# Feed-forward products by Winograd's scheme: where the sums of blocks are formed, and how the residual is added

## The chip, the core and the metric

The kernel runs on one core of a Trainium2 chip. A core has a matrix engine (TensorE, in the profile PE, with its weight loads as PEld), three elementwise engines (VectorE or DVE, ScalarE or ACT, GpSimd or POOL) and a queue engine that issues transfers (SyncE or SP). Each engine works off its own list of instructions in order and waits on semaphores for the others. The metric is device microseconds (us) for one execution.

## The reference

One step of a hybrid encoder layer over 512 prompt tokens and 8 x 16 sample tokens (640 columns in the kernel), width 2048, with token mixers, an output projection and then a convolutional gated feed-forward network. The change is in the last part:

```python
D_FF = (D_MODEL * 11 // 4) // 128 * 128        # 5632
def conv_ffn(h, conv_past, w_up, conv_w, w_down):
    gp, val = jnp.split(h @ w_up, 2, axis=-1)
    gc, conv_new = causal_conv(gp, conv_past, conv_w)       # width 3
    return (jax.nn.silu(gc) * val) @ w_down, conv_new
...
    x = x + jnp.concatenate([o_gdn, o_fox, o_lru], axis=-1) @ p['w_out'][l]
    f_out, ffn_conv_new = conv_ffn(rmsnorm(x, p['norm_ffn_g'][l]), ffn_conv, p['ffn_w_up'][l],
                                   p['ffn_conv_w'][l], p['ffn_w_down'][l])
    x = x + f_out
...
    return rmsnorm(x, p['final_norm_g']), [jnp.stack(lst) for lst in outs]
```

## The kernel before

The feature axis lies on the 128 partitions and the tokens on the free axis, in two halves of 320 columns (HALF). A float32 product is made of three float32r products: each operand is split into a rounded part (hi, "wh" for weights) and the rest (lo, "wl"), and hi*hi, hi*lo and lo*hi are added in PSUM. The mixers and the output projection (about the first 1,240 us of the trace) are untouched apart from the DMA scratch size.

The feed-forward products go by Winograd's form of Strassen's scheme with seven block products P1 to P7 instead of eight. One step of `wino`, a "pair", takes a 4-block weight A11, A12, A21, A22 of 128x128 each and a 4-block operand B11, B12, B21, B22 of 128x320 each; it needs the weight sums S1 to S4 and the operand sums T1 to T4, and issues 21 matmuls of 320 columns (7 products x 3 parts), in the order of `SEQP`. There are 520 pairs:

- `up(f)`, 44 times with 8 pairs each: gate and value of one feature tile. When the seven sums stand in PSUM they are combined into C11 to C22 (tile x for the gate, v for the value); the gate goes through the normalisation's correction `corr`, the convolution (`conv`, line 257) and silu, is multiplied with the value, and the result goes to the DRAM tensor hT by a DMA from GpSimd.
- `down(i, end)`, 32 "visits" with 168 pairs in all: the 8 output feature pairs are visited in turn in four rounds, each time with the pairs that have come since (list `ends`): 2, 3, 3, 4, 5, 6, 7, 8 pairs in the first round (38), 51 and 47 in the next two, and 7, 6, 5, 4, 4, 3, 2, 1 (32) in the last. Each visit adds its result to the residual, which is loaded from and stored to the DRAM tensor x2 by SyncE.
- `plain`, at the end: the last pair of k tiles without the scheme, the sums of squares, and `finish`, the final norm.

`wino_x` makes an operand's T's and splits all seven blocks into hi and lo ("x" tiles); `form0` calls it for the 8 operands of `up`, and `form` for the 21 operands ("hops") of `down`, one after the other between the pairs of the visits, since a visit of n pairs needs the first n hops. `wino_w` loads one pair's weights ("w", SyncE queue), makes the S's ("ws") and splits: `next_w` keeps three pairs ahead of the products, and `wh` and `wl` have three buffers each, so that the split for a pair waits until the matrix engine has done the pair three before it.

Before the change `wino_w` makes S1, S2 and S4 on GpSimd (lines 1047, 1049, 1052, one after the other, each needing the one before) and S3 on VectorE (1048); hi is made by ScalarE in two copies (1050, 1053) and lo by VectorE in two subtractions of 384 and 512 columns (1051, 1054). `wino_x` makes all T's on GpSimd (1013 to 1016). GpSimd also does the two multiplications by `corr` in `up` (1354, 1359) and three of the additions at the end of a visit of `down` (1415).

PSUM has eight banks for these products (`pf`); a group uses seven. The next group starts in the eighth and takes each of the others when its sum has been read, so it waits for VectorE's (and, for P1, ScalarE's) reads at the end of a group. Generators (`drive`) set which work is issued between which pairs, and a scheduler then sets the order of the instructions on each engine when the kernel is built.

## Time and profile before

| | |
|---|---|
| runs | 3004.94 us median of 3 (3001.29, 3005.12, 3004.94) |
| profiled execution | span 3000.6 us from the first to the last instruction; its whole time is not shown apart, and the fastest run lies 0.7 us above this span |
| mean granted TensorE clock | 0.983 |
| busy | PE 2888.2 us (96%), DVE 2315.5 (77%), ACT 1109.7 (37%), POOL 1631.7 (54%) |
| HBM | read 306.75 MB, written 59.39 MB, 122 GB/s over the span |

"Busy" is the union of an engine's instructions. A window's row gives the busy time of each engine within a stretch of the span, with the number of instructions in brackets (a few matmul records are missing), the granted clock and the share of the DMA engines. A row of a group gives how often an instruction occurred, its busy time, the mean nanoseconds of one, and the idle time of its engine just before it with the releaser. By the matmuls, `up` runs from about 1,240 to 2,330 us, `down` from there to about 2,940 us, `plain` and `finish` after it.

### The profile page before, as it was taken

To read this page: it belongs to the slowest core of one execution; us is meant where nothing else is said; L and a number is where in the kernel's file an instruction comes from. 1 tells how busy PE (TensorE), PEld (TensorE's weight loads), DVE (VectorE), ACT (ScalarE), POOL (GpSimd) and SP (SyncE) were. 2 spreads that over 40 slices of the span, in tenths; PEclk is the share of its full clock that TensorE was granted. 3 is DMA by queue.
4 is the path that set the end of the run, shared out by engine and by line. 5 is a ranking of instruction groups with operands and counts; after the bars stand their busy time and mean duration, and the time that the engine had idled before them with its cause. 6 is when DMAs were issued, how large, how long until landed. Compare 5 with 4: busy or idle time off the path is not lost. (4 is left out here: it accounts for less than half of the span.)

```text
span 3000.6 us, 54322 instructions
## 1 busy us (share of the span) xinstructions
PE 2888.2 (96%) x19927; PEld 2804.4 (93%) x19927; DVE 2315.5 (77%) x3976; ACT 1109.7 (37%) x2023; POOL 1631.7 (54%) x2367
## 2 busy tenths in 40 slices
PE   8999999999999999999999999999999789999997
PEld 7999999999999999999999999999999789999996
DVE  8746545645634537899999999999999988999888
ACT  4333323323322313444444443444444334434433
POOL 3312200310300014677777777777777988888775
PEclk9999999999999999999999999999999899999998
DMA  5123143134134745433333333333333555555443
GB/s 207 56 93 109 59 143 121 59 123 143 58 109 150 264 130 179 130 105 98 98 99 101 98 98 103 99 101 98 98 98 98 171 160 156 164 163 173 155 138 119
DMA packets 175772, 369.68 MB, mean 123 GB/s; under 512 B 20137, under 2 KB 25145, under 8 KB 175505
## 3 DMA queue, kind: packets, MB, share of 16 engines
q1 hardware_dynamic: 169088, 340.28, 36.4%
q0 software_dynamic: 6416, 25.94, 2.4%
q8 instruction: 156, 2.56, 0.4%
q14 instruction: 112, 0.91, 0.1%
HBM read 306.75 MB, written 59.39 MB: 122 GB/s over the span
## 5 line engine op out<-in xcount | busy, mean ns | idle before, releaser
L1077 PE MATMUL p<-x,wh 128*128 128x320 f32 x7280 | 1625.0, 312 | 45.0 <-DVE t L1412 31.9
L1077 PEld LDWEIGHTS p<-x,wh 128*128 128x128 f32 x7280 | 1230.5, 190 | 56.4 <-DVE t L1412 36.2
L1077 PE MATMUL p<-x,wl 128*128 128x320 f32 x3640 | 1138.9, 313 | 8.9 <-DVE wl L1054 5.2
L1077 PEld LDWEIGHTS p<-x,wl 128*128 128x128 f32 x3640 | 691.5, 190 | 19.9 <-DVE wl L1054 15.1
L1054 DVE TENSOR_TENSOR wl<-ws,wh 128x512 fp32r<-128x512 f32 x520 | 527.4, 1014 | 25.3 <-ACT wh L1053 25.2
L1051 DVE TENSOR_TENSOR wl<-w,wh 128x384 fp32r<-128x384 f32 x520 | 449.6, 865 | 73.4 <-ACT wh L1050 67.7
L1053 ACT CAST wh<-ws 128x512 fp32r<-128x512 f32 x520 | 321.6, 619 | 389.4 <-POOL ws L1052 340.1
L146 PE MATMUL d<-xh,whi 128*128 128x320 f32 x1536 | 396.8, 327 | 0.0
L1050 ACT CAST wh<-w 128x384 fp32r<-128x384 f32 x520 | 264.8, 509 | 330.0 <-issue 169.8
L1052 POOL TENSOR_TENSOR ws<-w,ws 128x128 f32<-128x128 f32 x520 | 352.7, 678 | 40.4
L146 PE MATMUL d<-xl,whi 128*128 128x320 f32 x1536 | 370.8, 310 | 0.0
L146 PE MATMUL d<-xh,wlo 128*128 128x320 f32 x1536 | 370.5, 310 | 0.0
L1047 POOL TENSOR_TENSOR ws<-w 128x128 f32<-128x128 f32 x520 | 284.1, 546 | 150.3 <-DVE wl L1054 144.0
L1049 POOL TENSOR_TENSOR ws<-ws,w 128x128 f32<-128x128 f32 x520 | 344.0, 662 | 37.5
L135 DVE TENSOR_TENSOR wlo<-raw,whi 128x512 fp32r<-128x512 f32 x230 | 175.1, 761 | 212.5 <-ACT whi L134 204.8
L134 ACT CAST whi<-raw 128x512 fp32r<-128x512 f32 x230 | 142.4, 619 | 405.9 <-PE d L146 354.1
L146 PEld LDWEIGHTS d<-xh,whi 128*128 128x128 f32 x1536 | 256.9, 190 | 9.5 <-issue 5.5
L146 PEld LDWEIGHTS d<-xl,whi 128*128 128x128 f32 x1536 | 262.6, 189 | 0.2 <-issue 0.2
L146 PEld LDWEIGHTS d<-xh,wlo 128*128 128x128 f32 x1536 | 262.7, 189 | 0.0
L1048 DVE TENSOR_TENSOR ws<-w 128x128 f32<-128x128 f32 x520 | 218.3, 426 | 13.2 <-DMA w<-in_w_down 0.7
L868 POOL COPY q<-t 128x128 f32<-128x128 f32 x24 | 12.1, 523 | 261.2 <-DVE t L220 139.8
L257 DVE SCALAR_TENSOR_TENSOR t<-t,prm,t 128x656 f32<-128x656 f32 (+1 forms) x136 | 138.4, 1017 | 6.5 <-ACT t L253 3.5
(395 smaller groups left out, 3513.5 us busy)
## 6 DMA issues: line engine op xcount, KB each, us to landing
w<-in_w_up SPq DMA_DIRECT2D x352, 256.0 KB, 2.6
raw<-in_w_in SPq DMA_DIRECT2D x196, 256.0 KB, 2.8
w<-in_w_down SPq DMA_DIRECT2D x184, 256.0 KB, 2.7
t<-x SPq DMA_DIRECT2D x74, 320.0 KB, 3.6
kc<-in_ckT SPq DMA_DIRECT2D x32, 512.0 KB, 5.0
vc<-in_cv SPq DMA_DIRECT2D x32, 512.0 KB, 5.8
x<-t SPq DMA_DIRECT2D x48, 320.0 KB, 2.2
hT<-t POOLq DMA_DIRECT2D x44, 320.0 KB, 2.5
```

The costliest lines, as they stand in the source:

```text
L134: nc.scalar.copy(hi[:, :n], raw[:, :n])
L135: nc.vector.tensor_sub(lo[:, :n], raw[:, :n], hi[:, :n].bitcast(F32))
L146: self.nc.tensor.matmul(ps[h][:, :HALF], wt[:, w], x[:, h * HALF:(h + 1) * HALF], start=start and i == 0, stop=stop and i == 2)
L1047: nc.gpsimd.tensor_add(s[:, 0], w[:, 0], w[:, 3])
L1048: nc.vector.tensor_sub(s[:, 2], w[:, 1], w[:, 0])
L1049: nc.gpsimd.tensor_sub(s[:, 1], s[:, 0], w[:, 1])
L1050: nc.scalar.copy(hi[:, 0:3], w[:, 1:4])
L1051: nc.vector.tensor_sub(lo[:, 0:3], w[:, 1:4], hi[:, 0:3].bitcast(F32))
L1052: nc.gpsimd.tensor_sub(s[:, 3], w[:, 2], s[:, 1])
L1053: nc.scalar.copy(hi[:, 3:7], s)
L1054: nc.vector.tensor_sub(lo[:, 3:7], s, hi[:, 3:7].bitcast(F32))
L1077: nc.tensor.matmul(ps[p], l[:, wi], r[:, xi], start=i == 0 and j == 0, stop=i == n - 1 and j == 2)
```

## The change

- The S's are made by VectorE alone, in place behind the loaded blocks of a wider w tile, in three instructions: two S's at once (128x256, one operand repeated), then two of 128x128 that each need the one before. The first row of blocks has the other sign (this shows in `combine` as subtractions), and the DRAM layout of the weights has another order of blocks. hi and lo are made of all seven blocks at once (one ScalarE copy and one VectorE subtraction of 128x896, where there were two of each). The S's and hi of the next pair are issued before lo of this one; raw weights are loaded further ahead (w has 5 buffers).
- The T's are made by VectorE, in three instructions, in a 7-block f tile (2 buffers, where there were 3 of 4 blocks); the split is in two pieces instead of three.
- `combine` is used by `up` and `down`. The two multiplications by corr move from GpSimd to VectorE.
- `down` no longer loads the residual. It combines into y and adds by an accumulating DMA from GpSimd: y onto x2 in DRAM, or in the last round x2 onto y in SBUF. Three GpSimd additions, one VectorE addition, 64 loads and 48 stores of SyncE per kernel go; 64 DMAs of GpSimd come.
- The DMA scratch of the GpSimd queue is 4096 instead of the default, and the load of the old convolution state fc0 is cut into four.

The order of the products, and the f tile:

```diff
-    SEQP = ((1, 0, 0), (6, 4, 5), (7, 5, 6), (5, 3, 4), (2, 1, 2), (4, 2, 1), (3, 6, 3))
+    SEQP = ((1, 2, 2), (6, 5, 6), (7, 4, 4), (5, 3, 5), (2, 0, 0), (4, 1, 3), (3, 6, 1))
...
-        return self.ffn.tile([P, 4, HALF], F32, tag="f", bufs=3, name=self.name("f"))
+        return self.ffn.tile([P, 7, HALF], F32, tag="f", bufs=2, name=self.name("f"))
```

`wino_x`:

```diff
-        nc.gpsimd.tensor_sub(t[:, 0], f[:, 1], f[:, 0])
-        nc.gpsimd.tensor_sub(t[:, 1], f[:, 3], t[:, 0])
-        nc.gpsimd.tensor_sub(t[:, 2], f[:, 3], f[:, 1])
-        nc.gpsimd.tensor_sub(f[:, 1], f[:, 2], t[:, 1])
+        nc.vector.tensor_tensor(f[:, 4:6], f[:, 3:4].to_broadcast([P, 2, HALF]), f[:, 1:3], op=OP.subtract)
+        nc.vector.tensor_sub(f[:, 6], f[:, 1], f[:, 5])
+        nc.vector.tensor_sub(f[:, 3], f[:, 0], f[:, 6])
...
+        for a, b in ((0, 3), (3, 7)):
+            nc.scalar.copy(h3[:, a:b], f[:, a:b])
+            yield
+            nc.vector.tensor_sub(l3[:, a:b], f[:, a:b], h3[:, a:b].bitcast(F32))
+            yield
```

The weights (`wino_raw` loads, `wino_w` sums and makes hi, `wino_lo` makes lo):

```diff
+    def wino_w(self, w, plain):
...
+        part = w[:, 0:4] if plain else w[:, 1:8]
+        if not plain:
+            nc.vector.tensor_tensor(w[:, 4:6], w[:, 0:1].to_broadcast([P, 2, P]), w[:, 2:4], op=OP.add)
+            nc.vector.tensor_add(w[:, 6], w[:, 4], w[:, 3])
+            nc.vector.tensor_add(w[:, 7], w[:, 1], w[:, 6])
...
+        nc.scalar.copy(hi[:, 0:n], part)
+        return part, hi, lo
...
+            now, raw = self.wn, self.next_raw()
+            self.wn = raw and self.wino_w(*raw)
+            self.wq.append(self.wino_lo(*now))
```

`combine`, for `up` and `down`:

```diff
+        nc.scalar.copy(u1, ps[1])
+        nc.vector.tensor_sub(u2, ps[6], u1)
+        nc.vector.tensor_add(c21, u2, ps[7])
+        nc.vector.tensor_add(u2, u2, ps[5])
+        nc.vector.tensor_add(c22, c21, ps[5])
+        c11(u1, ps[2])
+        nc.vector.tensor_add(c21, c21, ps[4])
+        c12(ps[3], u2)
```

`up`, then `down`:

```diff
-            nc.gpsimd.tensor_mul(x[:, 2:], x[:, 2:], corr[:, 2:])
+            nc.vector.tensor_mul(x[:, 2:], x[:, 2:], corr[:, 2:])
...
-            nc.gpsimd.tensor_mul(y[:, :656], y[:, :656], corr[:, 2:])
+            nc.vector.tensor_mul(y[:, :656], y[:, :656], corr[:, 2:])
...
-                nc.sync.dma_start(xs[e], x2[2 * i + e])
...
-            gadd(1, 1, u3)
-            gadd(1, 0, u3)
-            gadd(0, 1, u2)
-            if not last:
-                for e in range(2):
-                    nc.sync.dma_start(x2[2 * i + e], xs[e])
+                if last:
+                    nc.gpsimd.dma_start(y[e], x2[2 * i + e], accum_op=OP.add)
+                else:
+                    nc.gpsimd.dma_start(x2[2 * i + e], y[e], accum_op=OP.add)
```

GpSimd within one feature tile of `up`, before (t are the x, y and v tiles of `up`; ws the S's; the groups of three for the other pairs follow alike):

```order
L1354 TENSOR_TENSOR t_13241<-t_13241,corr 128x656 [waits DVE_49]
L1355 COPY ns_fc<-t_13241 128x2 [waits Pool_49]
L1356 COPY ns_fc<-t_13241 128x16
L1047 TENSOR_TENSOR ws_13345<-w_13344 128x128 [waits DMAHW1_49,DVE_49]
L1049 TENSOR_TENSOR ws_13345<-ws_13345,w_13344 128x128 [waits Pool_49]
L1052 TENSOR_TENSOR ws_13345<-w_13344,ws_13345 128x128 [waits Pool_49]
L1047 TENSOR_TENSOR ws_13379<-w_13378 128x128 [waits DMAHW2_49,DVE_49]
L1359 TENSOR_TENSOR t_13242<-t_13242,corr 128x656 [waits Activation_49]
```

and after, a whole feature tile:

```order
L1367 MEMSET t_18933 128x2 [waits DMASW4_49,Activation_49]
L1368 COPY t_18933<-ns_fc 128x8x2
L1380 COPY ns_fc<-t_18658 128x2 [waits DVE_49]
L1381 COPY ns_fc<-t_18658 128x16 [waits Pool_49]
L1392 DMA hT<-t_18660 128x640 [waits DVE_49]
```

All arithmetic has left the list; a memset, small copies and the DMA are what stays.

VectorE at the end of a feature tile of `up`, before (p are the PSUM sums, lines 1343 to 1352 the combining):

```order
L1048 TENSOR_TENSOR ws_21259<-w_21258 128x128 [waits DMAHW2_49,DVE_49]
L1051 TENSOR_TENSOR wl_21192<-w_21189,wh_21191 128x384 [waits PE_49,Activation_49]
L1054 TENSOR_TENSOR wl_21192<-ws_21190,wh_21191 128x512 [waits Activation_49]
L1347 TENSOR_TENSOR t_21224<-t_21224,p_20945 128x320 [waits PE_49,Activation_49]
L1048 TENSOR_TENSOR ws_21293<-w_21292 128x128 [waits DMAHW3_49,DVE_49]
L1348 TENSOR_TENSOR t_21225<-t_21224,p_20946 128x320 [waits DVE_49,PE_49]
L1343 TENSOR_TENSOR t_21223<-t_21224,p_20948 128x256 [waits DMASW6_49,PE_49]
L1349 TENSOR_TENSOR t_21224<-t_21224,p_20947 128x320 [waits DVE_49]
```

and after (lines 1106 to 1111 and 1374, 1375):

```order
L1047 TENSOR_TENSOR w_15573<-w_15573 128x256 [waits DMAHW4_49]
L1048 TENSOR_TENSOR w_15573<-w_15573 128x128 [waits DVE_49]
L1049 TENSOR_TENSOR w_15573<-w_15573 128x128 [waits DVE_49]
L1058 TENSOR_TENSOR wl_15579<-w_15483,wh_15578 128x896 [waits PE_49,Activation_49]
L1106 TENSOR_TENSOR t_15634<-p_15387,t_15634 128x320 [waits PE_49,Activation_49]
L1374 TENSOR_TENSOR t_15633<-t_15634,p_15390 128x256 [waits DMASW0_49,PE_49]
L1107 TENSOR_TENSOR t_15635<-t_15634,p_15388 128x320 [waits DVE_49]
L1375 TENSOR_TENSOR t_15633<-t_15634,p_15390 128x4x16
L1108 TENSOR_TENSOR t_15634<-t_15634,p_15389 128x320 [waits DVE_49]
L1109 TENSOR_TENSOR t_15635<-t_15635,p_15389 128x320
```

Three weight sums stand ahead of each lo, the later two directly behind what they need, as in 301 of 1,040 cases over the kernel; the combining is one block as before.

VectorE at the end of the first visit of `down`, before (t is the residual, u the sum of products):

```order
L1412 TENSOR_TENSOR t_26188<-t_26188,p_26192 128x320 [waits Activation_49]
L1418 TENSOR_TENSOR u_26283<-u_26283,p_26193 128x320
L1412 TENSOR_TENSOR t_26189<-t_26189,p_26195 128x320 [waits DMAHW7_49]
L1419 TENSOR_TENSOR u_26283<-u_26283,p_26194 128x320 [waits DVE_49]
L1412 TENSOR_TENSOR t_26188<-t_26188,p_26196 128x320
L1412 TENSOR_TENSOR t_26189<-t_26189,p_26197 128x320
```

and after, with the last of a hop's operand sums (f) ahead of it and weights for the next pairs behind it:

```order
L1022 TENSOR_TENSOR f_24828<-f_24828 128x320 [waits DVE_49]
L1106 TENSOR_TENSOR u_24836<-p_24756,u_24836 128x320 [waits PE_49,Activation_49]
L1047 TENSOR_TENSOR w_24690<-w_24690 128x256 [waits DMAHW1_49]
L1107 TENSOR_TENSOR t_24835<-u_24836,p_24757 128x320 [waits DMASW2_49,DVE_49,PE_49]
L1431 TENSOR_TENSOR t_24834<-u_24836,p_24759 128x320 [waits PE_49,Pool_49]
L1108 TENSOR_TENSOR u_24836<-u_24836,p_24758 128x320 [waits DVE_49]
L1109 TENSOR_TENSOR t_24835<-t_24835,p_24758 128x320
L1432 TENSOR_TENSOR t_24834<-p_24761,u_24836 128x320 [waits DVE_49,PE_49]
L1111 TENSOR_TENSOR t_24835<-t_24835,p_24760 128x320 [waits DVE_49]
L1048 TENSOR_TENSOR w_24690<-w_24690 128x128
L1058 TENSOR_TENSOR wl_24804<-w_24660,wh_24803 128x896
```

The wait for the residual's load (DMAHW) is gone; a wait for a GpSimd DMA that last read the y tile (DMASW) has come.

127 lines of the change are left out of this document (53 added, 74 removed).

## Prediction

> **What bounds the kernel now.** I read the page's busy rows first, then windows by stage, then the waits of the matrix engine, then the durations on VectorE.
>
> ```profile
> span 3000.6 us, 54322 instructions
> PE 2888.2 (96%) x19927; PEld 2804.4 (93%) x19927; DVE 2315.5 (77%) x3976; ACT 1109.7 (37%) x2023; POOL 1631.7 (54%) x2367
> DVE  8746545645634537899999999999999988999888
> POOL 3312200310300014677777777777777988888775
> PEclk9999999999999999999999999999999899999998
> ```
>
> The matrix engine is busy for 96%, and the change takes no matmul away. VectorE's 77% is a mean: from the 17th slice on, the feed-forward part, its digits are 8 and 9.
>
> ```profile
> core 0: us, PE busy (x) PEld busy (x) DVE busy (x) ACT busy (x) POOL busy (x), PEclk, DMA share, GB/s
> 1250.00:1300.00 50.00, 44.30 (x284) 42.55 (x284) 43.98 (x78) 21.91 (x38) 40.07 (x64) 0.97 0.30 88
> 1400.00:2200.00 800.00, 798.29 (x5398) 791.30 (x5397) 761.30 (x1252) 324.46 (x612) 616.68 (x998) 1.00 0.34 99
> 2320.00:2460.00 140.00, 112.78 (x658) 107.06 (x657) 129.08 (x189) 56.08 (x99) 126.42 (x156) 0.89 0.51 165
> 2460.00:2790.00 330.00, 309.99 (x2013) 304.00 (x2012) 296.12 (x445) 133.95 (x246) 280.41 (x380) 0.97 0.52 162
> 2790.00:2930.00 140.00, 140.00 (x957) 140.00 (x956) 118.75 (x210) 51.91 (x101) 102.25 (x162) 1.00 0.46 145
> ```
>
> In `up` (1400 to 2200) the matrix engine is full: 5398 recorded matmuls in 800 us, 0.148 us each, so a pair of 21 takes 3.11 us and a feature tile of 168 takes 24.9 us. That rate is the floor of every other stage. Against it 2320 to 2460 (the first round of `down`) lost 140 - 658 x 0.148 = 42.6 us, of which 27.2 are idle and the rest the clock of 0.89; 2460 to 2790 (second and third round) lost 330 - 2013 x 0.148 = 32.1; the start of `up` lost 50 - 284 x 0.148 = 8.0; the last round lost nothing. About 83 us can be had in all, 75 of them in `down`.
>
> ```profile
> engine line waited for: us in total, times, longest us
> PE p L1077 <- DVE t L1412: 31.9, 16, 3.5
> PE p L1077 <- ACT wh L1050: 5.1, 3, 2.3
> PE p L1077 <- DVE t L1347: 3.3, 1, 3.3
> PE p L1077 <- DVE wl L1051: 3.2, 4, 2.1
> ```
>
> These are the matrix engine's waits from 2320 to 2800. Most are for line 1412, VectorE's reading of a visit's sums out of PSUM, 16 times at about 2 us: VectorE, in order, comes to the end of a visit too late. GpSimd is in the same state there (126.42 of 140). So the question is whether VectorE with more work is done sooner.
>
> **VectorE's prices.** Seven rows with minimum, median and maximum of one line's instructions, and two groups of the window 1400 to 2200 with the mean behind the busy time:
>
> ```profile
> engine op xcount: duration ns min/median/max, first and last start us, forms
> L1054 DVE TENSOR_TENSOR wl<-ws,wh x520: 676/946/2114, 1227.0 to 2930.3; 128x512 fp32r<-128x512 f32 x174
> L1051 DVE TENSOR_TENSOR wl<-w,wh x520: 543/812/1760, 1226.5 to 2929.3; 128x384 fp32r<-128x384 f32 x174
> L1028 DVE TENSOR_TENSOR x<-f,x x29: 1145/1147/1408, 1156.3 to 2788.7; 128x960 fp32r<-128x960 f32 x29
> L1025 DVE TENSOR_TENSOR x<-f,x x29: 809/1080/1499, 1154.4 to 2786.3; 128x640 fp32r<-128x640 f32 x29
> L1412 DVE TENSOR_TENSOR t<-t,p x144: 472/475/482, 2363.6 to 2838.9; 128x320 f32<-128x320 f32 x144
> L1362 DVE TENSOR_TENSOR t<-t,t x88: 410/422/684, 1281.1 to 2368.5; 128x256 f32<-128x256 f32 x88
> L257 DVE SCALAR_TENSOR_TENSOR t<-t,prm,t x136: 895/982/1797, 58.1 to 2362.6; 128x656 f32<-128x656 f32 x88, 128x664 f32<-128x664 f32 x48
> L1343 DVE TENSOR_TENSOR t<-t,p 128x256 f32<-128x256 f32 x64 | 26.4, 412 | 0.0
> L1344 DVE TENSOR_TENSOR t<-t,p 128x64 f32<-128x64 f32 x64 | 13.6, 212 | 0.0
> ```
>
> Instructions that read two SBUF tiles spread widely (line 1054 from 676 to 2114 ns), those with an operand in PSUM not at all (line 1412 from 472 to 482). The timeline shows why:
>
> ```profile
> 1900.09 0.68 DVE L1054 TENSOR_TENSOR wl<-ws,wh 128x512 fp32r<-128x512 f32 x1
> 1900.80 0.29 DVE L1048 TENSOR_TENSOR ws<-w 128x128 f32<-128x128 f32 x1
> 1900.85 0.57 POOL L1047 TENSOR_TENSOR ws<-w 128x128 f32<-128x128 f32 x1 [1.38 <-DVE wl L1054]
> 1901.37 1.35 POOL L1359 TENSOR_TENSOR t<-t,corr 128x656 f32<-128x656 f32 x1
> 1901.39 1.74 DVE L1051 TENSOR_TENSOR wl<-w,wh 128x384 fp32r<-128x384 f32 x1 [0.30 <-ACT wh L1050]
> ```
>
> Line 1054 took 0.68 with GpSimd idle. Line 1051 began with GpSimd's 1.35 us multiplication and took 1.74, more than three times its 0.54 minimum: it waited the other out. With no arithmetic on GpSimd I take the minima: 128 columns 0.29, 256 columns 0.42, 640 columns 0.81, 960 columns 1.15. Between 512 (0.68) and 960 a column costs 1.05 ns, so 896 columns come to 1.08, 656 to 0.83, 320 from SBUF to 0.49, 1280 to 1.48. The upper bound is the medians under contention, which would add some 40%.
>
> The Trainium skill speaks against the change here: "Perfetto Trace Analysis", section Optimizing Scalar/DVE Operations, advises to move work from a saturated VectorE to ScalarE or even GpSimd. The same section warns that the two share a read port, so that this may not help, and "SBUF — State Buffer", section Who interferes with whom, says that an instruction with two SBUF inputs contends with a GpSimd instruction that reads SBUF. The trace agrees with the latter (0.68 against 1.74 in the rows above).
>
> A row's duration is also not what the queue pays:
>
> ```profile
> 2617.22 0.47 DVE L1412 TENSOR_TENSOR t<-t,p 128x320 f32<-128x320 f32 x1
> 2617.62 0.47 DVE L1418 TENSOR_TENSOR u<-u,p 128x320 f32<-128x320 f32 x1
> 1143.12 0.17 DVE L115 SCALAR_TENSOR_TENSOR s<-s,s 128x5 f32<-128x5 f32 x1
> 1143.32 0.17 DVE L117 SCALAR_TENSOR_TENSOR s<-s,s 128x5 f32<-128x5 f32 x1
> ```
>
> The second pair of sums starts 0.40 after the first: an independent instruction costs its duration less 0.07 or 0.08. Line 117, which needs what line 115 just wrote, starts 0.03 after its end. So a direct dependence costs 0.11 more; 301 of the 520 pairs' 1040 short sums stand so in the order, 0.06 us a pair.
>
> **The change, part by part.** *A pair's weights on VectorE:* 0.42 + 0.29 + 0.29 + 1.08 = 2.08, less 4 x 0.077, plus 0.06: 1.83 us. The three old lines in 2320 to 2790 took 1.03, 0.83 and 0.56 (groups of that window, next fence), 2.30 with the overlaps taken off. More work, less time, because the contention goes.
>
> ```profile
> L1054 DVE TENSOR_TENSOR wl<-ws,wh 128x512 fp32r<-128x512 f32 x127 | 131.0, 1032 | 18.5 <-ACT wh L1053 18.5
> L1051 DVE TENSOR_TENSOR wl<-w,wh 128x384 fp32r<-128x384 f32 x128 | 106.2, 829 | 17.8 <-ACT wh L1050 17.8
> L1048 DVE TENSOR_TENSOR ws<-w 128x128 f32<-128x128 f32 x127 | 68.6, 559 | 1.6
> ```
>
> *`up`.* A tile: 8 weights 16.6; combining 5 x 0.475 + 2 x 0.41 + 2 x 0.21 = 3.6; the two multiplications by corr 1.66; the convolution's two steps 1.8; the products with the gate 2 x 0.42 + 2 x 0.21 = 1.3. That is 25.0 in 49 instructions; less 49 x 0.077, plus 0.5 for dependences: 21.7 of 24.9 us, 87%, where the window shows 95% (761.30 of 800). `up` lost 1.7 us in 800 at 95%, so it stays bound by the matrix engine, gaining 1 to 2 us. Combining keeps its place and releases the banks within about 3 us as before.
>
> *`down`.* Combining is 7 x 0.40 = 2.8 us on VectorE (8 x 0.40 before). A hop costs 0.81 + 0.49 + 0.49 + 1.15 + 1.48 less 5 x 0.077, 4.0 us; before, its three subtractions alone were about 3.1. Second and third round: 98 pairs x 1.83 + 16 visits x 2.8 + 13 hops x 4.0 = 276 us against 98 x 3.11 = 305 for the matrix engine, 90%. By the old prices it was 98 x 2.30 + 16 x 3.2 + 13 x 3.1 = 317: VectorE was the bound, and stops being it. I leave 5 of the 32.1 us for visits with a hop of their own: plus 27. First round: 38 x 1.83 + 8 x 2.8 + 7 x 4.0 = 120 against 118; the short first visits are the worst, since the last feature tile's combining, a visit's combining and a hop (11 us of VectorE and more) fall on 6 us of matmuls. Following the order through the first five visits I find stalls of about 3, 2, 1, 1 and 1 us, and as much again for the slower clock behind them: 16 of the 42.6 stay, plus 26 or 27. For the clock, the Trainium skill ("TensorE: Matmul & The Clock Gate", part 1) has it halve only after an idle window of some 3.4 us; by that these short stalls would cost themselves alone, an estimate of 8 us better. The windows disagree: 0.97 from 2460 to 2790 with no listed stall above 3.5.
>
> *Start of `up`, 1140 to 1300.* Eight hops bring 8 x 1.6 = 13 us more onto VectorE, and the slowed subtractions get faster by about as much; 0, between -5 and +5. *ScalarE:* one copy of 896 columns instead of 509 + 619 ns, less in all; nothing, its cover is its 59% of idle time. *SyncE:* 112 transfers fewer and two reloads of a tile more, hidden behind three pairs of raw weights ahead (9 us).
>
> *Accumulating DMAs.* No row shows one. Nearest:
>
> ```profile
> hT<-t POOLq DMA_DIRECT2D x44, 320.0 KB, 2.5
> t<-x SPq DMA_DIRECT2D x74, 320.0 KB, 3.6
> ```
>
> A store takes 2.5 us to land, a load 3.6; bounds 2.5 and, read and write in turn twice over, 12. The y tile is written again two visits later, at least 15 us in the first round, so both ends cost nothing; a gain isn't in it either, as no VectorE row waited for the old loads. At the end the last tile lands 3 us of combining plus 3 to 12 after the last visit, and is read after 7 x 12 matmuls, 12.4 us: 0, at worst 4 lost. The smaller scratch and the cut load lie on GpSimd, which has 46% idle already: 0, at worst 3.
>
> *Sum:* 27 + 26.5 + 1.5 + 0 = 55 us. The profiled span 3000.6 becomes 2946; the runs' median 3004.94, 4.3 above that span (the fastest run 0.7), becomes 2950.
>
> **Rivals.** *VectorE becomes the bound of `up`* (slower). It decides at the overlap: 25.0 us in 49 instructions stay under 24.9 only while each starts at least a few ns before the last one's end. If waits made each cost +0.03 as behind line 115, a tile took 26.5: 44 x 1.6 = 70 us, and `down` would gain nothing: 3075. For it: nearly all new instructions carry a wait. Against it: line 1418 has waits too and overlaps.
>
> *The contention isn't what goes* (slower, same mechanism from another cause): at the old medians lo costs 0.95 + 0.81 and the sums 0.43 each, a pair 3.2 and a tile above 33 us; 44 x 8 = 350 more. That gives 3355. The 1.74 us row speaks against it. The advice of the Trainium skill's "Perfetto Trace Analysis" quoted above would come out here, were its warning not true.
>
> *`down` stays bound by VectorE.* If hops and combining still collide, only half of the 75 comes: 20 to 35 gained, about 2977. For it: the first round is 120 against 118, and GpSimd and VectorE together lost more there than sums of either explain.
>
> *Accumulations land late.* From 15 us on, the early visits wait; at 30 us visits 3 to 5 lose some 14 + 11 + 5, and 25 us of gain are left: 2980. Nothing in the rows above comes near.
>
> *All stalls go*, the start's too: 83 gained, 2922.
>
> **How the numbers follow.** Forecast (35 to 70 gained) 0.64; `down` half bound 0.14; all gone 0.10; `up` bound 0.05; contention stays 0.02; late accumulations 0.05. Two tenths of a per cent, 6 us, is about what a measurement of this kernel can tell. Faster holds the forecast, all gone, most of the half-bound and of the late case: 0.90; same 0.03; slower the two VectorE cases: 0.07. The range takes the forecast and half-bound cases and part of all gone: 2925 to 2985.
>
> **What would show it.** In the profile after: VectorE's lo of 896 columns near 1.08 us with a narrow spread, the 320-column PSUM rows still 0.475; VectorE near 87% in `up` with 0.148 us per matmul; the waits for a visit's reading of PSUM in `down` under 15 us instead of 32; matmuls of 2320 to 2460 up from 658 towards 850; the clock there back above 0.95; accumulating stores landing under 12 us. Wrong would make it: a lo above 1.3 us, VectorE above 97% in `up`, or waits for the GpSimd queue ahead of the combining.

## The result, and the profile after

The changed kernel takes 2919.55 us (median; 2916.72 to 2920.93), the kernel before 3005.03 on the same chip: a ratio of 0.9716, with a 95% interval of 0.9702 to 0.973. The forecast was 2950 with a range from 2925: the sign was right, but 85 us came where 55 were promised, and the measured time lies just under the range.

The page after, its busy rows and three of the slice rows:

```profile
span 2918.3 us, 51439 instructions
PE 2851.7 (98%) x19927; PEld 2781.9 (95%) x19927; DVE 2179.0 (75%) x4610; ACT 1057.5 (36%) x1474; POOL 411.3 (14%) x574
DVE  8746644635644445898888889988888999988877
POOL 4311310301310001010111101110101010000014
PEclk9999999999999999999999999999999999999998
```

GpSimd's digits of 7 and 8 have become 0 and 1, the clock row has lost all but its last 8, and VectorE is a little less busy although it took over most of GpSimd's sums. The windows that the prediction used, after:

```profile
core 0: us, PE busy (x) PEld busy (x) DVE busy (x) ACT busy (x) POOL busy (x), PEclk, DMA share, GB/s
1250.00:1300.00 50.00, 48.01 (x325) 47.15 (x324) 46.90 (x110) 22.09 (x26) 7.55 (x16) 1.00 0.37 111
1400.00:2200.00 800.00, 800.00 (x5457) 800.00 (x5456) 707.81 (x1593) 305.56 (x358) 84.21 (x162) 1.00 0.35 100
2320.00:2460.00 140.00, 136.01 (x906) 133.92 (x906) 137.53 (x286) 61.57 (x69) 16.50 (x20) 0.99 0.66 164
2460.00:2790.00 330.00, 327.62 (x2189) 320.75 (x2188) 284.79 (x593) 126.95 (x143) 29.73 (x34) 1.00 0.57 138
```

Look at the second row first. In 800 us of `up` there are now 5457 matmuls, 59 more than before, though PE's busy time was 798.29 then and is 800.00 now. So a matmul takes 0.1466 us (0.1467 as the mean over the 42 tiles below), a pair 3.08, a tile 24.64, and the 0.148 us that the prediction took for the floor contained lost time. PE's busy row hid it: a matmul is shown as 0.31 us long, with a modelled end, while the next one starts 0.147 us after it, so a start that comes 0.1 us late leaves no gap. The PEld row showed it: 791.30 of 800 before, 800.00 now. From 2320 to 2460 the window holds 906 matmuls instead of 658, at a clock of 0.99 instead of 0.89, and VectorE is still full there (137.53 of 140).

VectorE's prices (line, tiles, shape, count, then busy time and mean ns of one, then idle time before them):

```profile
L1058 DVE TENSOR_TENSOR wl<-w,wh 128x896 fp32r<-128x896 f32 x520 | 567.0, 1090 | 115.5 <-ACT wh L1053 74.0 <-PE p L1094 40.5
L1047 DVE TENSOR_TENSOR w<-w 128x256 f32<-128x256 f32 x520 | 218.8, 423 | 53.5 <-DMA w<-in_w_down 49.6 <-DMA w<-in_w_up 3.2
L1048 DVE TENSOR_TENSOR w<-w 128x128 f32<-128x128 f32 x520 | 149.6, 290 | 4.1
L1032 DVE TENSOR_TENSOR x<-f,x 128x1280 fp32r<-128x1280 f32 x29 | 43.3, 1492 | 0.0
L1379 DVE TENSOR_TENSOR t<-t,corr 128x656 f32<-128x656 f32 x44 | 37.1, 843 | 0.0
L1109 DVE TENSOR_TENSOR t<-t,p 128x320 f32<-128x320 f32 x68 | 32.9, 484 | 0.0
```

They are the forecast ones within 2%: 1.09 for 1.08 us (896 columns), 0.42, 0.29, 1.49 for 1.48, 0.84 for 0.83, and 0.484 for 0.475 with an operand in PSUM. The matrix engine's waits for VectorE and ScalarE in the scheme's products, from 2290 to 2900, longest groups:

```profile
PE p L1094 <- DVE u L1106: 2.9, 4, 0.9
...
PE p L1094 <- ACT wh L1053: 2.3, 1, 2.3
```

Before, VectorE's reading of PSUM alone was waited for 31.9 us in a shorter stretch. Where the gain came from is seen best by stages. The matmul records of both traces are complete for the scheme's products (10920 in each), so the start of each stage is the start of the matmul with that number; "limit" is the stage's number of matmuls at 0.1467 us.

| stage, us | limit | before | after | gain | forecast |
|---|---|---|---|---|---|
| up to the first tile of `up` | - | 1232.9 | 1228.7 | 4.2 | 0 |
| first tile of `up` | 24.6 | 34.7 | 29.6 | 5.1 | 0 |
| 42 tiles of `up` | 1034.9 | 1047.5 | 1035.1 | 12.4 | 1.5 |
| last tile of `up` and first round of `down` | 141.6 | 189.2 | 149.0 | 40.2 | 26.5 |
| second and third round | 301.9 | 333.1 | 311.2 | 21.9 | 27 |
| fourth round | 98.6 | 98.6 | 101.3 | -2.7 | 0 |
| rest | - | 64.6 | 63.4 | 1.2 | 0 |
| span | | 3000.6 | 2918.3 | 82.3 | 55 |

### The profile page after: what moved, and what is told of

It is laid out like the page before. It is cut to its first block, busy times and chain, and to the rows that moved or that the text cites. A ratio compares the mean times of both kernels' runs of the same rounds, so it can differ in the third digit from the quotient of the medians.

```text
span 2918.3 us, 51439 instructions
## 1 busy us (share of the span) xinstructions
PE 2851.7 (98%) x19927; PEld 2781.9 (95%) x19927; DVE 2179.0 (75%) x4610; ACT 1057.5 (36%) x1474; POOL 411.3 (14%) x574
## 5 line engine op out<-in xcount | busy, mean ns | idle before, releaser
L1094 PE MATMUL p<-x,wh 128*128 128x320 f32 x7280 | 1606.4, 309 | 8.6 <-DVE u L1106 2.9
L1094 PEld LDWEIGHTS p<-x,wh 128*128 128x128 f32 x7280 | 1215.6, 188 | 19.1 <-DVE u L1106 5.5
L1094 PE MATMUL p<-x,wl 128*128 128x320 f32 x3640 | 1121.4, 309 | 0.5 <-DVE wl L1058 0.5
L1053 ACT CAST wh<-w 128x896 fp32r<-128x896 f32 (+1 forms) x536 | 502.1, 937 | 980.5 <-PE p L1094 708.1
L1058 DVE TENSOR_TENSOR wl<-w,wh 128x896 fp32r<-128x896 f32 (+1 forms) x536 | 579.5, 1081 | 117.8 <-ACT wh L1053 76.2
L1047 DVE TENSOR_TENSOR w<-w 128x256 f32<-128x256 f32 x520 | 218.8, 423 | 53.5 <-DMA w<-in_w_down 49.6
L1049 DVE TENSOR_TENSOR w<-w 128x128 f32<-128x128 f32 x520 | 150.7, 291 | 6.2
L1048 DVE TENSOR_TENSOR w<-w 128x128 f32<-128x128 f32 x520 | 149.6, 290 | 4.1
L1438 POOL DMA_DIRECT2D x<-t x48 | 42.1, 1023 | 385.6 <-DVE t L1432 359.7
L1032 DVE TENSOR_TENSOR x<-f,x 128x960 fp32r<-128x960 f32 (+1 forms) x58 | 76.7, 1325 | 2.5 <-ACT x L1030 2.5
L1030 ACT CAST x<-f 128x960 fp32r<-128x960 f32 (+1 forms) x58 | 64.1, 1126 | 31.4 <-DVE f L1022 13.3
```

What stands on the lines that cost most here:

```text
L1030: nc.scalar.copy(h3[:, a:b], f[:, a:b])
L1032: nc.vector.tensor_sub(l3[:, a:b], f[:, a:b], h3[:, a:b].bitcast(F32))
L1047: nc.vector.tensor_tensor(w[:, 4:6], w[:, 0:1].to_broadcast([P, 2, P]), w[:, 2:4], op=OP.add)
L1048: nc.vector.tensor_add(w[:, 6], w[:, 4], w[:, 3])
L1049: nc.vector.tensor_add(w[:, 7], w[:, 1], w[:, 6])
L1053: nc.scalar.copy(hi[:, 0:n], part)
```

## The experiments

Two theories were held against each other. *Contention*: GpSimd's arithmetic, which reads SBUF, makes VectorE's SBUF instructions longer, and that goes. *Structure*: the old kernel lost its time in the chain itself, by sums that went through GpSimd's queue and back, by lo's that waited for hi copies of the same pair, by more and shorter instructions. Each run has its own runs of the kernel before beside it; the stages of the profiled runs that matter below (us; each stage is read from one profiled execution):

| kernel | median | ratio to before (95%) | 42 tiles of `up` | last tile | round 1 | round 2 | round 3 |
|---|---|---|---|---|---|---|---|
| before | 3005.0 | 1 | 1047.5 | 32.4 | 156.8 | 176.7 | 156.4 |
| changed | 2919.6 | 0.9716 (0.9702 to 0.973) | 1035.1 | 24.6 | 124.4 | 162.6 | 148.5 |
| pool_reads | 3463.9 | 1.1527 (1.1508 to 1.1546) | 1408.5 | 24.6 | 124.8 | 163.1 | 148.1 |
| pool_writes | 3010.2 | 1.0015 (1.0004 to 1.0027) | 1121.9 | 24.6 | 124.5 | 163.5 | 147.5 |
| reads_paced | 3043.2 | 1.0136 (1.0121 to 1.0151) | 1087.5 | 25.6 | 146.3 | 187.3 | 157.8 |
| writes_paced | 2953.4 | 0.9829 (0.9796 to 0.9862) | 1052.6 | 24.6 | 129.4 | 170.5 | 149.4 |
| before_S | 2984.2 | 0.994 (0.9925 to 0.9954) | 1041.1 | 31.2 | 151.4 | 173.9 | 153.8 |
| before_all | 2957.3 | 0.9846 (0.9829 to 0.9863) | 1037.4 | 24.6 | 152.6 | 167.6 | 149.5 |
| before_ahead | 2953.0 | 0.9826 (0.9812 to 0.9841) | 1043.7 | 24.6 | 146.3 | 164.8 | 147.6 |
| no_ahead | 2926.6 | 0.974 (0.9725 to 0.9754) | 1034.7 | 24.6 | 127.5 | 164.7 | 146.9 |
| two_lo | 2927.9 | 0.975 (0.9734 to 0.9767) | 1035.1 | 24.6 | 128.7 | 159.9 | 148.9 |
| no_accum | 2923.6 | 0.9731 (0.9716 to 0.9745) | 1035.0 | 24.6 | 131.3 | 159.0 | 145.4 |
| corr_on_pool | 2926.7 | 0.9744 (0.973 to 0.9759) | 1037.6 | 24.6 | 129.3 | 162.5 | 147.0 |
| xsums_on_pool | 2966.4 | 0.9875 (0.9858 to 0.9891) | 1035.0 | 24.6 | 140.2 | 173.8 | 151.9 |
| dve_384 | 2961.1 | 0.9855 (0.9841 to 0.987) | 1037.6 | 26.4 | 144.6 | 168.7 | 149.1 |
| w6n | 2914.9 | 0.9703 (0.9689 to 0.9718) | 1035.1 | 24.6 | 124.4 | 162.4 | 146.1 |
| hybrid | 2911.4 | 0.9696 (0.9682 to 0.971) | 1034.8 | 24.6 | 124.1 | 158.8 | 144.8 |
| hybrid2 | 2914.0 | 0.9699 (0.9684 to 0.9713) | 1035.5 | 24.6 | 124.5 | 158.3 | 144.9 |

An interval reaches about 0.0015 (4 to 5 us) to each side in most rows, so two kernels whose ratios lie within 0.003 of each other are hardly told apart. The rounds are counted as 38, 51 and 47 pairs in every row, for hybrid2 too, whose own first round has 40.

### GpSimd busy again, on nothing: pool_reads and pool_writes

```diff
             nc.vector.tensor_add(w[:, 7], w[:, 1], w[:, 6])
+            for _ in range(3):
+                nc.gpsimd.tensor_add(self.dmy, self.ident, self.ident)   # pool_writes: nc.gpsimd.memset(self.dmy, 0.0)
```

> The changed kernel with three additions of 128x128 on GpSimd for each pair, constants in, a scratch tile out, on which nothing depends. Contention (GpSimd reading SBUF slows VectorE): before, three such additions went with about 0.27 us more on each of three VectorE instructions of a pair; the same again makes a pair 1.83 + 0.8 = 2.6 us, a tile 28 against 24.6, so VectorE bounds up and down both: 3030 to 3090 us, lo of 896 columns at 1.4 us or more and widely spread. Rival, structure (the old kernel lost its time by sums that went through GpSimd's queue and back, and by raw weights loaded too late): nobody waits for these additions, so 2920 within 6.

> The changed kernel with three memsets of 128x640 on GpSimd for each pair, of about 0.63 us, which write SBUF and read nothing. If only GpSimd's reads contend: 2920 within 6 and lo of 896 columns still near 1.09 us. If any GpSimd activity in SBUF does, as in the run with additions: 3030 or more. Structure as the cause: 2920 within 6 too.

3463.9 and 3010.2 us, but not for either theory's reason. Nothing tied these instructions to a pair, so in the program's order they went far ahead: 1087 of the 1560 additions ran between 1400 and 2200, beside only 16 stores of hT, in front of the halo copies of the tiles. One wait of ScalarE in that stretch, of pool_reads, tells it:

```profile
ACT t L1107 <- POOL ns_fc L1384: 281.5, 9, 40.6
```

The copy of P1, which begins the combining, waited nine times, 281.5 us in all, for a buffer that GpSimd's halo copy had yet to read, and the banks with it. So this run measures a queue, not contention: work on which nothing depends, put ahead of work on which something does, cost 544 us against the changed kernel. Of pool_writes one thing can be kept: its memsets overlapped nearly all of VectorE's instructions of the stretch, and lo still took 1085 ns.

### The same, paced: reads_paced and writes_paced

```diff
         nc.scalar.copy(hi[:, 0:n], part)
+        nc.scalar.copy(tok[:, :1], hi[:, 0, :1].bitcast(F32))            # tok: 8 buffers
+        nc.gpsimd.tensor_add(self.dmy, tok[:, :1].to_broadcast([P, P]), self.ident)
+        for _ in range(2):
+            nc.gpsimd.tensor_add(self.dmy, self.dmy, self.ident)
# writes_paced: tensor_copy(self.dmy[:, :1], tok[:, :1]), then three times memset(self.dmy, 0.0) of 128x512
```

> The changed kernel with the same three 128x128 additions on GpSimd, now begun for each pair by a number that ScalarE writes behind the pair's hi copy, so that they stand beside that pair and not far ahead of it; nothing depends on them. Contention: in the unpaced run an overlapped sum of 128 columns took 0.37 to 0.46 us instead of 0.29 and a lo up to 1.23 instead of 1.09, so a pair 1.83 + 0.45 and a tile 25.5 against 24.6; up loses some 40 us, the first round 17, the second and third 15: 2970 to 3020. Structure: 2921 within 6.

> The same with three memsets of 128x512 (about 0.5 us each) in place of the additions, begun in the same way. If GpSimd's reads alone contend: 2921 within 6. If what cost 90 us in the unpaced run was GpSimd's writing and not the place of its queue: 2970 or more.

Reads: 3043.2 us, 124 above the changed kernel, more than its whole gain and 23 above the expected range, though nothing waits for the additions. The window 1400 to 2200 and VectorE's groups in it, of reads_paced:

```profile
1400.00:2200.00 800.00, 788.26 (x5187) 763.93 (x5186) 787.85 (x1515) 333.77 (x588) 634.62 (x893) 1.00 0.33 96
```

```profile
L1063 DVE TENSOR_TENSOR wl<-w,wh 128x896 fp32r<-128x896 f32 x247 | 267.0, 1081 | 1.4 <-ACT wh L1053 1.4
L1047 DVE TENSOR_TENSOR w<-w 128x256 f32<-128x256 f32 x248 | 131.1, 529 | 5.5 <-DMA w<-in_w_up 4.2
L1049 DVE TENSOR_TENSOR w<-w 128x128 f32<-128x128 f32 x248 | 111.8, 451 | 3.1
L1048 DVE TENSOR_TENSOR w<-w 128x128 f32<-128x128 f32 x248 | 93.5, 377 | 2.1
```

VectorE is at 98.5% and bounds `up`: a tile takes (1087.5 / 42) 25.9 us; 25.5 was expected. The sums went from 423, 290 and 291 ns to 529, 377 and 451; lo itself did not grow. The single instructions of the window show the rule: the 125 sums of 256 columns that began while an addition was under way took 644 ns on average, the 61 during which an addition began 412, and the 62 that met none 411. So an instruction that begins while GpSimd reads waits for it, and one that has begun is not stretched. Lo's mean stayed because only 34 of its 247 began during an addition (1,100 ns; in pool_reads it was 39, with 1,237). The sums of 320 columns with an operand in PSUM took 474 ns when they began during an addition (141 of them), 472 otherwise (9).

Writes: 2953.4 us, neither of the two expected values. The durations say that GpSimd's writes do not touch VectorE (the same groups, of writes_paced):

```profile
L1063 DVE TENSOR_TENSOR wl<-w,wh 128x896 fp32r<-128x896 f32 x257 | 279.1, 1086 | 76.6 <-ACT wh L1053 76.4
L1047 DVE TENSOR_TENSOR w<-w 128x256 f32<-128x256 f32 x257 | 106.9, 416 | 4.3 <-DMA w<-in_w_up 4.0
L1049 DVE TENSOR_TENSOR w<-w 128x128 f32<-128x128 f32 x257 | 73.2, 285 | 3.2
L1048 DVE TENSOR_TENSOR w<-w 128x128 f32<-128x128 f32 x257 | 72.9, 284 | 2.1
```

Yet 34 us were lost, because the contention has a second side. The one-column copy of the token reads SBUF, and this is its duration (minimum, median, maximum, ns):

```profile
L1056 POOL COPY dmy<-tok x536: 176/285/13929, 1222.3 to 2938.7; 128x1 f32<-128x1 f32 x179
```

It takes 0.18 us at the least; while VectorE issues one instruction behind the other it waited up to 13.9 us for its turn. In the 188 copies longer than 0.5 us VectorE was busy for 99% of the time, with no gap longer than 0.104 us; in the 216 of at most 0.2 us it was busy for 59%. GpSimd was thereby busy for 734.80 of 800 us, and the halo copy of two columns took 1,679 ns on average instead of 189. That this is what cost the 34 us is argued and not measured apart, and the four runs spread from 2942.8 to 2963.8. Taken as the price of the queue and the token in reads_paced too, where GpSimd was less busy (634.62), it leaves, as an estimate, 90 of the 124 us to the reads: as much as the whole gain.

### One part alone: before_S, before_all, before_ahead

The first moves the three sums of weights to VectorE, the second also the four T's, the two corr products and the three residual sums, the third also makes sums and hi copies a pair ahead of the lo's:

```diff
-        nc.gpsimd.tensor_add(s[:, 0], w[:, 0], w[:, 3])
+        nc.vector.tensor_add(s[:, 0], w[:, 0], w[:, 3])
...
-        nc.gpsimd.tensor_sub(t[:, 0], f[:, 1], f[:, 0])
+        nc.vector.tensor_sub(t[:, 0], f[:, 1], f[:, 0])
...
+            now, src = self.wn, next(self.wseq, None)
+            self.wn = src and self.wino_w(*src)
+            self.wq.append(self.wino_lo(*now))
```

> The kernel before with one part of the change: the three sums of weights of a pair that GpSimd had go to VectorE, everything else stays (the T's, the corr products and the residual sums on GpSimd, raw weights as before). VectorE then has 4 x 0.29 + 0.68 + 0.54 less the overlaps, 2.1 us a pair, with GpSimd busy for some 25% instead of 77%. Contention or chain, both say that most of the gain comes from here: 2935 to 2960; if the weights are but half of it and the rest hangs on the prefetch, the T's and the residual: 2965 or more.

> The kernel before with all of its elementwise work between the last mixer and the tail moved from GpSimd to VectorE (weights, T's, corr, residual sums) and nothing else: the old order of a pair, two lo's of 512 and 384 columns, raw weights, loads and stores of the residual as they were. Contention: VectorE needs 6 instructions of 2.38 us less overlaps, 2.0 us a pair, 11 sums a visit (4.5) and 4.0 a hop, so up becomes 1035 to 1040 us, the first round 131 to 145, the second and third together 305 to 320: 2930 to 2950. Structure (the hi copies and sums a pair ahead, one lo, three raw pairs ahead carry the gain): little better than the run with the weights alone, 2965 to 2985.

> The kernel before with all elementwise work of the feed-forward part on VectorE (2957 us) and the look-ahead alone added: sums and hi copies of a pair one pair ahead of its two lo's, raw weights, buffers, T's, residual as before. If the look-ahead is the rest of the gain: the first round 152.6 becomes 132 to 138, the second 167.7 becomes 160, the whole 2925 to 2937. If raw prefetch, fewer instructions and the residual carry it: 2950 to 2957.

before_S gained 19 us, far below its range, for by both theories the weights were most of it. The lo of 512 columns shows why (minimum, median, maximum):

```profile
L1054 DVE TENSOR_TENSOR wl<-ws,wh x520: 675/685/2109, 1225.9 to 2911.7; 128x512 fp32r<-128x512 f32 x174
```

The median is the uncontended 0.685, but those that meet a corr product wait it out (65 of the 259 between 1400 and 2200 took 1.76 us on average), and in `down` the T's and residual sums on GpSimd hit VectorE's sums of weights, of which there are now more (403 ns from 2338 to 2663 for line 1047). The sums of weights are 981 of the 1,350 us of arithmetic that GpSimd had in the feed-forward part, so moving nearly three quarters of the contending work brings less than a quarter of the gain. before_all takes the rest of GpSimd's arithmetic away and comes to 2957.3 (26 more, 7 above the range that contention gave): `up` and its last tile are then within 2.5 us of the changed kernel, but the first round stays at 152.6. before_ahead adds the look-ahead: 2953.0, outside the range for "the rest of the gain", inside that for "others carry it"; the first round gains 6.3, and `up` gives as much back (1043.7 instead of 1037.4).

### One part undone: no_ahead, two_lo, no_accum

```diff
-            now, raw = self.wn, self.next_raw()           # no_ahead
-            self.wn = raw and self.wino_w(*raw)
-            self.wq.append(self.wino_lo(*now))
+            self.wq.append(self.wino_lo(*self.wino_w(*raw)))
...
-        self.nc.vector.tensor_sub(lo[:, 0:n], part, hi[:, 0:n].bitcast(F32))      # two_lo; the hi copy likewise
+        for s in (slice(0, 3), slice(3, n)):
+            self.nc.vector.tensor_sub(lo[:, s], part[:, s], hi[:, s].bitcast(F32))
...
+            for e in range(2):                            # no_accum: eleven sums, store by SyncE
+                nc.sync.dma_start(y[e], x2[2 * i + e])
-                    nc.gpsimd.dma_start(x2[2 * i + e], y[e], accum_op=OP.add)
+                    nc.sync.dma_start(x2[2 * i + e], y[e])
```

> The changed kernel without its look-ahead on the chip: a pair's sums, hi copy and lo are again issued in one step, not the sums and the hi copy a pair ahead of the lo (raw weights still three pairs ahead). With all arithmetic on VectorE in the old structure the time was 2957 against 2924 for the new one with the old residual, so 34 us hang on structure. If it is the look-ahead: VectorE waits at each lo for ScalarE, the first round 124 becomes 135 to 145, the whole 2935 to 2952. If it is not: 2920 within 5.

> The changed kernel with the hi copy and the lo of a pair in two parts of 384 and 512 columns as before, in place of one of 896. VectorE pays 0.56 + 0.69 - 0.08 instead of 1.09, some 0.08 us a pair, ScalarE one more instruction: the first round 124 becomes 127, the whole 2920 to 2926. If the merging was what shortened VectorE's queue (the fixed cost of more instructions, waits among them): 2930 or more.

> The changed kernel with the residual of a visit loaded ahead by SyncE, eleven sums on VectorE (the three that stood on GpSimd among them) and stored by SyncE, instead of seven sums and the accumulating DMAs. If the lighter combining matters: 32 visits with four sums more, 1.7 us each, of which the first round, where VectorE is busy for 98.9%, pays all 8 (14 us) and the others a part: 2930 to 2945. If the contention is all: 2920 within 6.

They lose 7, 8 and 4 us, the largest part in the first round of the profiled runs (3.1, 4.3 and 6.9); only the interval of two_lo lies clear of the changed kernel's. The look-ahead is not the missing 34: no_ahead lies between its two outcomes, nearer to the lower; two_lo is 2 above the range of the mere price; no_accum is inside that of "the contention is all". What the three leave open is seen when the first round of before_ahead and of no_accum, which have the same eleven sums and the look-ahead both, are laid beside each other. Before_ahead, then no_accum:

```profile
2328.00:2474.50 146.50, 128.06 (x801) 123.18 (x801) 143.53 (x380) 62.94 (x111) 1.47 (x4) 0.95 0.56 183
```

```profile
2320.00:2451.00 131.00, 122.04 (x798) 118.47 (x797) 130.43 (x279) 54.54 (x62) 2.41 (x4) 0.99 0.61 198
```

VectorE is full in both, without contention in either, so the round lasts as long as VectorE's work in it: 380 instructions against 279. A pair has six there and four here (1.88 against 1.75 us from start to start), and eight hops of about 4 us end in before_ahead's round against six in no_accum's, which had formed two by its start, before_ahead one. Two hops and 38 x 0.13 us make 13 of the 15 us between the rounds. That reading comes from counts in the traces; no run moved the hops alone.

### Back on GpSimd, with data: corr_on_pool and xsums_on_pool

```diff
-            nc.vector.tensor_mul(x[:, 2:], x[:, 2:], corr[:, 2:])            # corr_on_pool, and the second product
+            nc.gpsimd.tensor_mul(x[:, 2:], x[:, 2:], corr[:, 2:])
...
-        nc.vector.tensor_sub(f[:, 6], f[:, 1], f[:, 5])                       # xsums_on_pool, and the two sums around it
+        nc.gpsimd.tensor_sub(f[:, 6], f[:, 1], f[:, 5])
```

> The changed kernel with the two products with corr of a feature tile (656 columns) back on GpSimd. VectorE is spared 1.66 us a tile and pays up to 1.35 us twice for instructions that meet them: in up its 88% stays below 93%, so 2920 within 5 by contention. If the convolution, which waits for the first product, then comes late for the banks of the next tile: 2935 or more.

> The changed kernel with the three sums of a hop (640, 320, 320 columns, SBUF to SBUF) back on GpSimd. VectorE is spared 1.6 us a hop. By contention it pays for what meets 3 to 4 us of GpSimd work, some 2 to 3 us, and the hop's operands come 2 us later: the first round 124 becomes 128 to 140, the whole 2923 to 2945. Without contention the spared 7 x 1.6 us would shorten the first round, where VectorE is full: 2912 to 2920.

The corr products cost 7 us where contention gave at most 5; `up` pays 2.5 and the first round 5. The hop's sums cost 47, nearly twice the upper end. 16 of them are lost by the end of `up`'s first tile, before any accumulating DMA: for each of the first eight operands GpSimd takes 4.8 us (2.31 + 1.22 + 1.26), VectorE 1.8. In the first three rounds (30 us) VectorE is not the bound (125.67 of 140 us from 2334 to 2474, 285.06 of 330 from 2460 to 2790), so its longer instructions are not the main cause there. GpSimd's waits from 2330 to 2800 show the place:

```profile
POOL x L1438 <- DVE t L1432: 159.8, 18, 17.3
POOL f L1020 <- DMA f<-hT: 105.3, 11, 12.6
```

The accumulating DMAs (line 1438) are issued in GpSimd's queue and wait there for a visit's combining; a hop's sums behind them wait as well, and ScalarE's copy of a hop waited for them 11.8 us in this stretch. How much of the 30 us this queue makes was not measured apart. In this kernel the new residual and the old place of these sums do not go together.

### Where VectorE becomes the bound: dve_384

```diff
             nc.vector.tensor_add(w[:, 7], w[:, 1], w[:, 6])
+            nc.vector.tensor_sub(self.dmy, w[:, 1:4].rearrange("p a c -> p (a c)"), w[:, 4:7].rearrange("p a c -> p (a c)"))
```

> The changed kernel with one more independent VectorE subtraction of 384 columns for each pair, 0.54 us less the overlap of 0.08, with nothing waiting for it. By the prediction's sum a tile of up comes to 21.7 + 8 x 0.46 = 25.4 us of VectorE against 24.64 of the matrix engine: up 1035 becomes 1067 and more, the first round 124 becomes 141, the second and third 311 become 335: 3000 to 3020. If VectorE had more slack than the sum says (instructions overlap more when there are more of them): 2960 or less.

```profile
1400.00:2200.00 800.00, 799.96 (x5450) 798.99 (x5450) 799.94 (x1849) 304.50 (x358) 406.27 (x162) 1.00 0.34 101
```

2961.1, near the lower outcome. VectorE is full (799.94 of 800), and yet a tile of `up` takes 24.70 us, not 25.4. From start to start an instruction costs here what it costs in the changed kernel: 0.202 us for 128 columns and 0.335 for 256 in both, 1.002 for lo against 1.008. Only the durations are shown about 0.01 us longer, and overlap by as much more (0.097 us instead of 0.087). Added up so, a tile is 8 x 1.741 for the weights, 6.98 for the rest and 8 x 0.468 for the new instruction: 24.65. The prediction's sum was 0.7 us a tile too high at the bound because it took off 0.077 for each overlap, and because it added 0.5 for direct dependences: in this full queue all but one of the 1,847 instructions start before the one ahead of them has ended. The changed kernel stands one instruction of 384 columns a pair away from the bound. The first round lost 20 us for 38 x 0.46 = 17.5 of work: no slack there.

### Attempts at a faster one: w6n, hybrid, hybrid2

```diff
-            nc.vector.tensor_add(w[:, 7], w[:, 1], w[:, 6])
+            nc.vector.tensor_add(w[:, 0], w[:, 1], w[:, 6])      # w6n: w tile of 7 blocks, 6 buffers, 4 raw pairs ahead
...
+            if not acc:                                           # hybrid: w6n, and in rounds 2 and 3
+                return (yield from down_load(i, end, make))       # the residual as in no_accum
...
-        ends = [2, 3, 3, 4, 5, 6, 7, 8] + ...
+        ends = [2, 3, 4, 5, 5, 6, 7, 8] + ...                     # hybrid2
```

> The changed kernel with the fourth sum of weights written over the block that only the first sums need, so that a raw weight tile takes 3.5 KB instead of 4, six of them instead of five, and four pairs of raw weights ahead instead of three. VectorE waited 49.6 us for w_down behind 2440. If those waits end on the matrix engine's path (the second to fourth round lost 5.6 + 3.7 + 2.7 us): 2908 to 2914. If VectorE's slack covers them: 2919 within 4.

> An attempt to beat both: six smaller raw weight tiles as in w6n, accumulating DMAs only in the first round of down, where VectorE is full, and in the last visits, whose tile stays on chip; in the visits between, the residual is loaded, summed on VectorE and stored as in no_accum, since there the accumulating transfers went with 49.6 us of waits for weights against 8.3. First round 124 as in w6n, second to fourth 159 + 145 + 100: 2905 to 2912. If the waits for weights are covered anyway: 2915 within 3.

> The hybrid kernel with the pairs of the first round of down set at 2, 3, 4, 5, 5, 6, 7, 8 instead of 2, 3, 3, 4, 5, 6, 7, 8. VectorE is full in the first round; longer early visits give the same combinings and hops two pairs of matmuls more to lie beside. If that is what holds the first round: its loss of 7 us becomes 3 to 5, the whole 2907 to 2910. If the hops' operands come too late for the longer visits: 2912 to 2918.

VectorE's largest wait behind the first round in the changed kernel (2440 to 2760), in no_accum (2450 to 2756) and in hybrid (2441 to 2745), in this order:

```profile
DVE w L1047 <- DMA w<-in_w_down: 33.7, 30, 2.4
```

```profile
DVE w L1047 <- DMA w<-in_w_down: 2.2, 4, 0.9
```

```profile
DVE w L1047 <- DMA w<-in_w_down: 3.0, 4, 1.5
```

w6n alone, with one more buffer, is on the edge between its two outcomes. The waits for weights go with the accumulating DMAs (w6n, which keeps them, still has 25.6 us in 27 waits from 2440 to 2750). Hybrid accumulates only where VectorE is full and in the last visits: 2911.4, and its second and third round, 158.8 and 144.8 us, lie at 157.1 and 144.8 of matmuls. It is 8 us below the changed kernel, though the intervals overlap (0.9682 to 0.971 against 0.9702 to 0.973). hybrid2 brought nothing: its first 38 pairs take 124.5 us, and its own first round of 40 pairs 130.7, 7.5 above its matmuls, where hybrid's 124.1 lies 7.0 above. Its time is that of the outcome expected second, but not for the reason given there: none of the matrix engine's waits in that round is for a hop, and VectorE is as full as before (129.39 of 130.7 us).

## Why the prediction was right or wrong

*The mechanism: right, and shown, for about half of the gain.* GpSimd's reads lengthen VectorE's instructions (644 instead of 411 ns for 256 columns); writes do not (416); operands in PSUM are not concerned (474 and 472). The Trainium skill's "SBUF — State Buffer" (Who interferes with whom) agrees with these numbers of the paced runs; the advice of "Perfetto Trace Analysis" to move work towards GpSimd would have cost here what reads_paced shows (124 us).

*The prices, `up` at 87%: right* (88.5%: 707.81 of 800).

*The floor of 0.148 us a matmul: the step that failed.* "In `up` the matrix engine is full" was read from PE's 798.29 of 800. The true time is 0.1467, and the lost 8.7 us of the window stood in the PEld number of the same row. The prediction's own last row contradicted the floor as well: 957 matmuls in 140.00 us, 0.1463 each. So 42 tiles gained 12.4 and not 1.5, and "About 83 us can be had" was 101 (the stages before less their limits: 10 + 13 + 48 + 31); "*All stalls go*" at 2922 was built on the same floor. The trace before shows where most of these stalls were. 41 times in the 42 tiles a matmul waited for a lo of line 1054. One case, with rows of GpSimd, VectorE and the matrix engine:

```profile
1402.10 1.35 POOL L1359 TENSOR_TENSOR t<-t,corr 128x656 f32<-128x656 f32 x1
1402.12 1.75 DVE L1051 TENSOR_TENSOR wl<-w,wh 128x384 fp32r<-128x384 f32 x1 [0.30 <-ACT wh L1050]
1405.27 0.68 DVE L1054 TENSOR_TENSOR wl<-ws,wh 128x512 fp32r<-128x512 f32 x1
1406.00 0.42 PE L1077 MATMUL p<-x,wl 128*128 128x320 f32 x1
1406.26 0.46 PE L1077 MATMUL p<-x,wh 128*128 128x320 f32 x2
```

The lo of line 1051 waited out GpSimd's product with corr, that of line 1054 came late behind it, and the two matmul starts of the last rows follow the ones ahead by 0.23 and 0.25 us instead of 0.147. All late starts of the 42 tiles (over 0.17 us behind the one ahead) add up to 12.8 us before and to 0.2 after. before_S and before_all bring 6.4 and 10.1 us of the 12.4: most of the hidden stalls went with GpSimd's arithmetic. But before_ahead, without that arithmetic, has 41 such waits again, so the order on VectorE counts as well.

*What the 27 us above the forecast consist of (profiled spans).* The floor accounts for 10.9 in the 42 tiles, and the floor and the windows' edges together for 5.0 in the last tile and first round, where 47.6 could be had instead of 42.6; a remaining loss put too high there (16 instead of 7.4) for 8.7; the start, put at nothing, for 9.3; the rest for 1.2. Against it stand 5.1 too little in the second and third round and 2.7 lost in the fourth. With the floor alone put right in `up` the forecast would have been 2939, inside the range: it took the mis-sized remaining loss and the start as well to leave it.

*The first round: mis-sized.* "16 of the 42.6 stay" was 8 of stalls and 8 of the clock behind them; 7.3 stayed (124.4 against 117.1). The windows were not the stages either: before, the last tile of `up` ended at 2347.5 and the first round at 2504.3, so some of the loss booked to 2460 to 2790 was the first round's. The clock's share is a real mechanism. Before, at the second pair of the round, and after, at its worst stall (start, duration, matmuls):

```profile
2354.35 0.90 PE L1077 MATMUL p<-x,wh 128*128 128x320 f32 x2 [3.28 <-DVE t L1347]
2355.05 0.47 PE L1077 MATMUL p<-x,wl 128*128 128x320 f32 x1
2355.32 0.73 PE L1077 MATMUL p<-x,wh 128*128 128x320 f32 x2
```

```profile
2327.58 1.09 PE L1094 MATMUL p<-x,wh 128*128 128x320 f32 x3 [2.33 <-ACT wh L1053]
2328.51 0.31 PE L1094 MATMUL p<-x,wl 128*128 128x320 f32 x1
```

Behind some stalls matmuls follow each other at 0.27 us. 87 did so in unbroken rows of 7 to 13 from 2315 to 2505 before (87 x 0.12 = 10.4 us), 7 from 2293 to 2443 after (0.8 us), where one stall alone was longer than 1.1 us. before_all has 65 in rows of 8 to 21 in its first round, and no two matmul starts there are more than 2.91 us apart. An idle window of some 3.4 us, as the Trainium skill has it ("TensorE: Matmul & The Clock Gate", part 1), is thus not needed for the slower clock here. The estimate by that page, 8 us better, was nearer than mine only because hardly a stall was left to slow the clock.

*Second and third round: plus 27 forecast, 21.9 came.* The matrix engine's waits for VectorE's reading of PSUM went from 31.9 us to 2.9, as forecast; that VectorE had been the bound before is weaker than it looked, since 1.03 + 0.83 + 0.56 less three overlaps is 2.19 and not 2.30, which makes the sum of 317 us about 306 against 305 for the matrix engine (VectorE was busy for 296.12 of 330 before, 284.79 after). But "so both ends cost nothing", said of the accumulating DMAs, missed what they do to others: in this stretch one lands after 5.8 us (within the bounds 2.5 to 12), and weights wait beside them. Without them the two rounds took 6.7 us less (no_accum), and the fourth, which lost 2.7 us with them, 1.8 less. "A gain isn't in it either" missed the other side: without the load, VectorE has four sums fewer a visit than no_accum, 6.9 us of the first round. Together plus 4, with intervals that overlap.

*Start of `up`: 0, between -5 and +5; 5.1 came in the first tile, and 4.2 ahead of it.* The operands' sums on VectorE are the likely cause of the 5.1: with these back on GpSimd (xsums_on_pool) the first tile takes 34.4 us again, against 34.7 before and 29.6 after. The smaller scratch and the cut load are not needed for the 4.2: before_all and before_ahead, which have neither, reach the first tile at 1230.1 and 1227.0, against 1232.9 before and 1228.7 after (one profile each).

*What carried the 85.* By runs: weights' sums 19, GpSimd's other arithmetic 26 more, merged lo 8, look-ahead 4 to 7, accumulating DMAs 4 (effects that need not add; those of 4 to 7 are within the noise). Some 20 us, nearly all in the first round, no run holds alone; fewer instructions and two hops fewer in it are what the traces show. The forecast gave the whole to contention, which moving the arithmetic alone (before_all, 46) only half bears out: in a stage where VectorE is full, each instruction saved counts as well.

*The rivals.* "VectorE becomes the bound of `up`" was one instruction of 384 columns a pair away (dve_384); "the contention isn't what goes" is refuted by reads_paced; the late accumulations did not come.
